# The priority of a recurrence's evictions in a hybrid diffusion layer: 60 places or 1500

## The chip, the cores and the metric

The kernel runs on one core of one Trainium2 chip. The metric is the device time of one execution in microseconds, measured over repeated runs; one further execution is taken by the hardware profiler.

## The reference

Two layers. Each projects the modulated, normalised stream into a convolution branch and a bidirectional RWKV-7 branch, joins both by an output projection and adds a SwiGLU network. Latents are 512 tokens, the context prefix 256, width 1024. What matters here is the recurrence, 8 heads of 64 by 64 state, run forwards and backwards, over the context first and from its states over the latents:

```python
def step(s, inp):
    r_t, k_t, v_t, w_t, kk_t, b_t = inp
    sa = -jnp.einsum("bhvk,bhk->bhv", s, kk_t)
    s = (s * w_t[:, :, None, :] + sa[..., None] * b_t[:, :, None, :]
         + v_t[..., None] * k_t[:, :, None, :])
    y = jnp.einsum("bhvk,bhk->bhv", s, r_t) if emit else None
    return s, y
```

```python
prep_c = rwkv_prep(uc[..., CONV_IN:], *rw)
yc, s_f, s_b = rwkv_scans(prep_c, s_zero, s_zero, emit=not last)
prep_x = rwkv_prep(ux[..., CONV_IN:], *rw)
yx, _, _ = rwkv_scans(prep_x, s_f, s_b, emit=True)
mix_x = jnp.concatenate([conformer_conv(ux[..., :CONV_IN], *cv),
                         rwkv_out(yx, prep_x, *post)], axis=-1).astype(x.dtype)
x = x + gt1 * (mix_x @ w_out[l])
x = x + gt2 * swiglu(modulate(rmsnorm(x, norm2_g[l]), sh2, sc2), ffn_wg[l], ffn_wu[l], ffn_wd[l])
```

## The kernel before

The recurrence is computed in chunks of 64 tokens. Heads come in 4 pairs, each pair has 12 chunks in 3 groups of four, so a layer has 12 blocks b (a pair and a group) and in each block 4 chain steps s, forwards and backwards side by side: 48 chain steps a layer. The stages of a block:

- `prep(b)` makes the decayed keys and receptances of a block, once for each direction: ScalarE and VectorE take turns over `tmp` and `tw` and end in `KR` and `bk`. The chunk products `grams(b)` on TensorE read these and are masked by VectorE into `G`.
- `base(b)` inverts the 16 by 16 diagonal blocks. `G` goes to memory (`d`), comes back as `Dt`, and VectorE runs 15 steps of two small instructions each (`xtmp`, then `XT`; the shapes run from 64x15 through 64x64 back to 64x15). ScalarE transposes the result, and SyncE's queue writes it to memory (`dimg`).
- `inverses` loads it as `Tm`, and `levels` extends it to 64 by 64 on TensorE, with evictions on ScalarE (`W`, `Tm`) and VectorE (`Tm`, lines 1004 and 1006).
- `tokens` turns keys and values into `tT` and `UV`.
- `chain(b, s)` is the step of the recurrence itself, and each of its matmul groups needs the eviction of the one before. `pz` (from `G` and `UV`) goes by ScalarE to `Z`; `pu` (from `Tm` and `Z`) goes by ScalarE and VectorE to the halves of `UV`; `pm` (from `tT` and `UV`) goes by VectorE to the state `S`, and two ScalarE copies put `S` into the next step's `UV`. These are the evictions that stand under `soon()`.

Beside them run the input projections (`pd` banks, evicted to `r`, `k`, `v`, `z`), the convolution, whose taps are VectorE instructions on `acc`, one for each tap (`conv`), the gating and early output projection (`mix_early`, `out_early`), and the split of each weight tile into `wh` (ScalarE) and `wl` (VectorE).

TensorE's order is written out by hand: `weave` lays all these generators into one order by a table of places, under a manual schedule of that engine alone. The order on ScalarE, VectorE, GpSimd and SyncE is set when the program is built, by a list scheduler that takes, by its own estimates of time, the ready instruction that was recorded first. `tc.high_priority(n)` lets the instructions under it count as if they had been recorded n places earlier. Each engine then runs its own instructions in that fixed order.

Of the kernel before, what the change touches and what calls it, by code (L numbers as in the profile page):

```python
# [181 lines left out]
def net(ctx: ExitStack, tc: tile.TileContext, I, out):  # L182
# [62 lines left out]
        PE.matmul(out=out, lhsT=lhsT, rhs=rhs, start=start, stop=stop)  # L245

    def soon():
        return tc.high_priority(60)

    def run(steps):  # L250
        for _ in steps:
# [350 lines left out]
    for l in range(DEPTH):  # L602
# [430 lines left out]
        def chain(b, s):  # L1033
# [18 lines left out]
            with soon():  # L1052
                act(Z, pz[:, 0:128])
# [16 lines left out]
            with soon():  # L1070
                act(UV[64:128, 2 * s_:2 * s_ + 2, 0, :], pu3[64:128], AF.Copy, scale=-1.0)
                ts(UV[0:64, 2 * s_:2 * s_ + 2, 1, :], pu3[0:64], -1.0, 0.0)
            yield

            if not fin:
                pm = bank("c")
                for d, hh in DH:
                    hs = slice(64 * hh, 64 * hh + 64)
                    mm(pm[hs, 64 * d:64 * d + 64], tT[:, hh, 2 * s_ + d, :], UV[:, 2 * s_ + d, hh, :])
                Sn = s2.tile([128, 2, 64], F32, tag="S", name=nm("S"))  # L1080
                with soon():
                    for d in range(2):
                        pd_ = pm[:, 64 * d:64 * d + 64]
                        if S is None:
                            ts(Sn[:, d, :], pd_, pc[:, d, s:s + 1], 0.0)
                        else:
                            stt(Sn[:, d, :], pd_, pc[:, d, s:s + 1], Q[:, d, :], MUL, ADD)

                    bn, sn = (b, s + 1) if s < 3 else (b + 1, 0)
                    Un = BS[bn]["UV"][sn // 2]  # L1090
                    act(Un[64:128, 2 * (sn % 2):2 * (sn % 2) + 2, 0, :], Sn[0:64])
                    act(Un[0:64, 2 * (sn % 2):2 * (sn % 2) + 2, 1, :], Sn[64:128])
                P["S"] = Sn
# [382 lines left out]
```

## Time and profile before

| | us |
|---|---|
| median of 3 runs (2222.3 to 2234.28) | 2222.33 |
| the profiled execution | 2218.84 |
| its span, first to last instruction | 2217.1 |
| mixing of layer 0, about | 140 to 620 |
| mixing of layer 1, about | 1345 to 1800 |
| VectorE, ScalarE, GpSimd busy | 1449.0, 940.3, 200.4 |

The profiled execution is 3.5 us below the median. Between the two mixing stretches lie the feed-forward network of layer 0 and the start of layer 1, and after the second one the feed-forward network of layer 1; no chain step runs there.

### The profile page before, as it was taken

The numbers are of one execution on the slowest core, as the hardware profiler recorded it, in microseconds if no ns is written. First come the engines' busy times: TensorE is split into PE (matmuls) and PEld (weight loads), VectorE is DVE, ScalarE is ACT, GpSimd is POOL, SyncE is SP. The second block draws the span as 40 slices with busy tenths as digits, with TensorE's granted clock in tenths as the row PEclk, the third lists the DMA queues.
The fourth block names the chain that finished last, engine by engine and source line by source line (L and its number), as shares of the span: only waits on it lengthen the run. The fifth ranks groups of instructions, "written<-read, shape, count | busy, mean of one in ns | idle before, by whom it ended". The sixth has DMA issues, their size and how long they took to land.

```text
span 2217.1 us, 44112 instructions
## 1 busy us (share of the span) xinstructions
PE 2057.2 (93%) x17578; PEld 1661.3 (75%) x17578; DVE 1449.0 (65%) x3286; ACT 940.3 (42%) x2184; POOL 200.4 (9%) x528
## 2 busy tenths in 40 slices
PE   5999999998998999999999999999999879999997
PEld 4777777776687888888888876667666568888886
DVE  5678888877758665565653766778877764433446
ACT  4455646555435212112112545576666443222223
POOL 0102131311010000000000000122212010000000
PEclk9999999999899999999999999999999999999998
DMA  8222232243551343343332413121214441333233
GB/s 296 70 75 71 80 78 74 65 107 117 157 195 61 123 132 126 118 139 124 122 116 92 137 40 76 32 62 47 70 33 108 123 158 58 95 97 102 86 98 121
DMA packets 197804, 226.32 MB, mean 102 GB/s; under 512 B 110560, under 2 KB 140000, under 8 KB 197472
## 3 DMA queue, kind: packets, MB, share of 16 engines
q1 hardware_dynamic: 196448, 221.42, 33.0%
q8 instruction: 138, 2.26, 0.4%
q10 hardware_dynamic: 1152, 2.10, 0.2%
q14 instruction: 66, 0.54, 0.1%
HBM read 196.62 MB, written 26.85 MB: 101 GB/s over the span
## 4 chain that ended last, share of the span: by engine, by line
PE 60%; DVE 12%; ACT 10%; issue 7%; DMA 7%; POOL 2%; SPq 0%; POOLq 0%; DVEq 0%; ACTq 0%
PE pd L245 30%; PE pw L245 23%; PE pc L245 5%; DMA at<-in_adaT 5%; ACT tmp L233 2%; DVE junk L236 2%; DVE wl L239 2%; ACT UV L233 1%; PE pw L936 1%; PE pw L412 1%; DVE acc L236 1%; ACT wh L233 1%; PE pw L924 1%; ACT W L233 1%; DVE xtmp L239 1%
## 5 line engine op out<-in xcount | busy, mean ns | idle before, releaser
L245 PE MATMUL pd<-h,wh 128*128 128x512 f32 (+3 forms) x2496 | 685.8, 364 | 10.3 <-ACT h L233 10.3
L233 ACT ACTIVATE wh<-raw 128x1024 fp32r<-128x1024 f32 (+2 forms) x234 | 220.8, 944 | 679.6 <-PE pw L245 281.1
L245 PEld LDWEIGHTS pd<-h,wh 128*128 128x128 f32 (+1 forms) x2496 | 425.9, 190 | 80.1 <-ACT h L233 11.8
L245 PE MATMUL pd<-h,wl 128*128 128x512 f32 (+3 forms) x1248 | 426.1, 364 | 2.7 <-DVE wl L239 2.7
L239 DVE TENSOR_TENSOR wl<-raw,wh 128x1024 fp32r<-128x1024 f32 (+2 forms) x234 | 253.8, 1085 | 134.6 <-ACT wh L233 133.6
L245 PE MATMUL pw<-h,wh 128*128 128x512 f32 (+1 forms) x1264 | 317.0, 350 | 3.9 <-DVE x L236 2.8
L245 PEld LDWEIGHTS pd<-h,wl 128*128 128x128 f32 (+1 forms) x1248 | 224.9, 190 | 37.7 <-DVE wl L239 3.8
L245 PEld LDWEIGHTS pw<-h,wh 128*128 128x128 f32 x1264 | 211.5, 190 | 38.9 <-DVE x L236 4.5
L236 DVE SCALAR_TENSOR_TENSOR junk<-at,cr 128x1024 bf16<-128x1024 f32 x112 | 137.0, 1224 | 130.7 <-DMA at<-in_adaT 129.4
L236 DVE SCALAR_TENSOR_TENSOR acc<-z,cw,acc 128x497 f32<-128x497 f32 (+20 forms) x216 | 193.1, 894 | 4.3 <-ACT acc L233 2.8
L245 PE MATMUL pw<-h,wl 128*128 128x512 f32 (+1 forms) x632 | 193.0, 351 | 0.0
L245 PE MATMUL pd<-mid,wh 128*128 128x512 f32 (+1 forms) x568 | 139.3, 348 | 8.5 <-ACT wh L233 2.9
L245 PE MATMUL pw<-mid,wh 128*128 128x512 f32 (+1 forms) x568 | 138.5, 347 | 1.1 <-ACT wh L233 1.1
L245 PEld LDWEIGHTS pw<-h,wl 128*128 128x128 f32 x632 | 107.4, 190 | 15.1
L245 PEld LDWEIGHTS pd<-mid,wh 128*128 128x128 f32 x568 | 94.9, 192 | 25.0 <-ACT wh L233 4.4
L245 PEld LDWEIGHTS pw<-mid,wh 128*128 128x128 f32 x568 | 95.4, 193 | 14.9 <-ACT wh L233 1.3
L1044 POOL TENSOR_TENSOR Q<-S,pc 128x128 f32<-128x128 f32 x80 | 49.5, 619 | 527.6 <-DVE S L236 210.1
L239 DVE TENSOR_TENSOR ft<-ft,pw 128x512 f32<-128x512 f32 (+1 forms) x67 | 37.7, 589 | 81.1 <-PE pw L245 80.8
L245 PE MATMUL pd<-mid,wl 128*128 128x512 f32 (+1 forms) x284 | 88.5, 351 | 2.3 <-DVE wl L239 2.2
L245 PE MATMUL pw<-mid,wl 128*128 128x512 f32 (+1 forms) x284 | 88.1, 349 | 0.2 <-DVE wl L239 0.2
L848 POOL MEMSET tmp<- 128x4 f32 x48 | 5.2, 108 | 891.5 <-PE pw L245 638.5
L239 DVE TENSOR_TENSOR xtmp<-XT,Dt 64x15 f32<-64x15 f32 (+4 forms) x360 | 74.9, 208 | 8.2 <-DMA Dt<-d 3.5
(207 smaller groups left out, 3166.5 us busy)
## 6 DMA issues: line engine op xcount, KB each, us to landing
raw<-in_wgu SPq DMA_DIRECT2D x88, 512.0 KB, 3.5
at<-in_adaT SPq DMA_DIRECT2D x56, 512.0 KB, 3.8
raw<-in_win SPq DMA_DIRECT2D x42, 512.0 KB, 3.4
ada<-in_ada SPq DMA_DIRECT2D x40, 512.0 KB, 4.7
raw<-in_wd SPq DMA_DIRECT2D x48, 320.0 KB, 2.8
Tm<-dimg SPq DMA_DIRECT2D x96, 128.0 KB, 2.8
raw<-in_wd SPq DMA_DIRECT2D x32, 384.0 KB, 3.0
d<-G SPq DMA_DIRECT2D x96, 64.0 KB, 2.1
```

The source lines that it names most:

```text
L233: A.activation(out=out, in_=in_, func=func, **k)
L236: V.scalar_tensor_tensor(out=out, in0=in0, scalar=scalar, in1=in1, op0=op0, op1=op1, **k)
L239: V.tensor_tensor(out=out, in0=a, in1=b, op=op)
L245: PE.matmul(out=out, lhsT=lhsT, rhs=rhs, start=start, stop=stop)
L412: PE.transpose(pt[:, c - c0:c - c0 + 128], wide[:, c:c + 128], ident)
L848: G.memset(lx[:, :, 0:1], 0.0)
L924: PE.transpose(pt[hh][:, o:o + 64], bk[hs, d, cc, hh:hh + 2, :].rearrange("p j t -> p (j t)"), ident[hs, hs])
L936: PE.transpose(pv[0:64, o:o + 128], src, ident)
L1044: G.tensor_tensor(out=Q, in0=S, in1=pc[:, :, s:s + 1].to_broadcast([128, 2, 64]), op=MUL)
```

## The change

The number of places by which the chain's evictions count as earlier goes from 60 to 1500. With 60 an eviction passes ready instructions that were recorded within a step or two of it; with 1500 it passes anything that is ready on its engine. No instruction is added or taken away.

```diff
     def soon():
-        return tc.high_priority(60)
+        return tc.high_priority(1500)
```

TensorE's order is the same in both kernels. Three places show what moves on the others.

ScalarE in layer 0, near 157 us. `UV<-S` are the two copies of the state, `Z` the eviction of the next step, `y` the chain's output, `z` the eviction of a projection; `tmp`, `tw` and `pc` belong to the prep of a later block. Rows with + stand there now, those with - stood there.

```order
 L233 ACTIVATE tw_1648<-pw_1644,der_147 128x256
+L233 ACTIVATE UV_1077<-S_1722 64x2x64 x2
 L233 ACTIVATE tmp_1647<-tmp_1647 128x4x64
 L233 ACTIVATE y_1555<-pc_1682 128x64 x2
+L233 ACTIVATE Z_1745<-pc_1740 128x128
 L233 ACTIVATE z_1832<-pd_1497 128x512
-L233 ACTIVATE UV_1077<-S_1722 64x2x64 x2
 L233 ACTIVATE tmp_1647<-tmp_1647 128x260 x2
-L233 ACTIVATE Z_1745<-pc_1740 128x128
+L233 ACTIVATE pc_1581<-tmp_1647 128x4
 L233 ACTIVATE tmp_1647<-tw_1648,der_147 128x4x64
-L233 ACTIVATE pc_1581<-tmp_1647 128x4
```

The copies have passed a `tmp`, the `y` pair and `z`; `Z` has passed `z` and the `tmp` pair.

VectorE in layer 1, near 1524 us, before. `XT` and `xtmp` are the inversion's steps, `bk` and the scan on `tmp` the prep's, `k` the shifted projection.

```order
L239 TENSOR_TENSOR xtmp_16276<-XT_16275,Dt_16274 64x39
L236 SCALAR_TENSOR_TENSOR bk_16520<-tw_16526,tmp_16525 128x256
L239 TENSOR_TENSOR XT_16275<-XT_16275,xtmp_16276 64x13x3
L242 TENSOR_SCALAR UV_15757<-pc_16619 64x2x64
L239 TENSOR_TENSOR xtmp_16276<-XT_16275,Dt_16274 64x28
L236 SCALAR_TENSOR_TENSOR k_16668<-pd_16338,prm,k_16668 128x511
L239 TENSOR_TENSOR XT_16275<-XT_16275,xtmp_16276 64x14x2
L236 SCALAR_TENSOR_TENSOR S_16641<-pc_16636,pc_15476,Q_16597 128x64
L239 TENSOR_TENSOR xtmp_16276<-XT_16275,Dt_16274 64x15
L236 SCALAR_TENSOR_TENSOR S_16641<-pc_16636,pc_15476,Q_16597 128x64
L239 TENSOR_TENSOR XT_16275<-XT_16275,xtmp_16276 64x15
L853 SCALAR_TENSOR_TENSOR tmp_16579<-one_95,tmp_16579 128x260
```

The same place in the changed kernel:

```order
L239 TENSOR_TENSOR xtmp_16276<-XT_16275,Dt_16274 64x55
L239 TENSOR_TENSOR bk_16520<-tmp_16525 128x4x64
L236 SCALAR_TENSOR_TENSOR S_16641<-pc_16636,pc_15476,Q_16597 128x64 x2
L239 TENSOR_TENSOR XT_16275<-XT_16275,xtmp_16276 64x11x5
L236 SCALAR_TENSOR_TENSOR bk_16520<-tw_16526,tmp_16525 128x4x64
L239 TENSOR_TENSOR xtmp_16276<-XT_16275,Dt_16274 64x48
L236 SCALAR_TENSOR_TENSOR k_16668<-pd_16338,prm,k_16668 128x511
L239 TENSOR_TENSOR XT_16275<-XT_16275,xtmp_16276 64x12x4
L236 SCALAR_TENSOR_TENSOR k_16668<-pd_16338,prm,k_16668 128x511
L239 TENSOR_TENSOR xtmp_16276<-XT_16275,Dt_16274 64x39
L853 SCALAR_TENSOR_TENSOR tmp_16579<-one_95,tmp_16579 128x260
```

The pair of `S` stood behind the `XT` of step 14 and now stands ahead of that of step 11; the last `XT` (64x15) has seventeen rows between itself and `S`.

VectorE in the last block of layer 1, near 1739 us, before. `acc` are the convolution's taps, `r` an eviction of the early output projection.

```order
L236 SCALAR_TENSOR_TENSOR S_19796<-pc_19791,pc_18597,Q_19735 128x64
L239 TENSOR_TENSOR XT_19373<-XT_19373,xtmp_19374 64x13x3
L236 SCALAR_TENSOR_TENSOR S_19796<-pc_19791,pc_18597,Q_19735 128x64
L239 TENSOR_TENSOR xtmp_19374<-XT_19373,Dt_19372 64x28
L239 TENSOR_TENSOR wl_19757<-raw_19753,wh_19755 128x768
L239 TENSOR_TENSOR XT_19373<-XT_19373,xtmp_19374 64x14x2
L236 SCALAR_TENSOR_TENSOR acc_19466<-z_18422,cw_13433,acc_19466 128x508
L239 TENSOR_TENSOR xtmp_19374<-XT_19373,Dt_19372 64x15
L236 SCALAR_TENSOR_TENSOR r_19751<-pd_19759,mod_10592,r_19751 128x512
L239 TENSOR_TENSOR XT_19373<-XT_19373,xtmp_19374 64x15
L236 SCALAR_TENSOR_TENSOR acc_19466<-z_18422,cw_13433,acc_19466 128x508
L239 TENSOR_TENSOR wl_19818<-raw_19814,wh_19816 128x768
```

The same place in the changed kernel, from `S` on:

```order
L236 SCALAR_TENSOR_TENSOR S_19796<-pc_19791,pc_18597,Q_19735 128x64 x2
L239 TENSOR_TENSOR xtmp_19374<-XT_19373,Dt_19372 64x63
L236 SCALAR_TENSOR_TENSOR acc_19466<-z_18422,cw_13433,acc_19466 128x507
L239 TENSOR_TENSOR XT_19373<-XT_19373,xtmp_19374 64x9x7
L239 TENSOR_TENSOR wl_19757<-raw_19753,wh_19755 128x768
L239 TENSOR_TENSOR xtmp_19374<-XT_19373,Dt_19372 64x60
L236 SCALAR_TENSOR_TENSOR acc_19466<-z_18422,cw_13433,acc_19466 128x508
L239 TENSOR_TENSOR XT_19373<-XT_19373,xtmp_19374 64x10x6
L236 SCALAR_TENSOR_TENSOR acc_19466<-z_18422,cw_13433,acc_19466 128x508
L239 TENSOR_TENSOR xtmp_19374<-XT_19373,Dt_19372 64x55
L236 SCALAR_TENSOR_TENSOR acc_19466<-z_18422,cw_13433,acc_19466 128x507
L239 TENSOR_TENSOR XT_19373<-XT_19373,xtmp_19374 64x11x5
```

`S` stood behind step 12 of the inversion and now stands behind step 8; sixteen more rows follow up to the last `XT` (eight of the inversion, six taps, an `r` and a second `wl`).

## Rows read from the trace of the kernel before

**Rows 1.** The page, part 1: busy time, share of the span, instructions.
```profile
PE 2057.2 (93%) x17578; PEld 1661.3 (75%) x17578; DVE 1449.0 (65%) x3286; ACT 940.3 (42%) x2184; POOL 200.4 (9%) x528
```

**Rows 2.** Windows, both mixing stretches: length, busy PE PEld DVE ACT POOL, clock, DMA.
```profile
140.00:620.00 480.00, 440.73 (x5773) 338.83 (x5773) 387.14 (x1013) 267.67 (x758) 96.90 (x224) 0.95 0.33 93
1345.00:1800.00 455.00, 414.00 (x5027) 296.24 (x5023) 327.11 (x948) 269.77 (x763) 85.06 (x234) 0.96 0.28 74
```

**Rows 3.** TensorE's waits, layer 0's mixing: us in total, times, longest.
```profile
PE pc L245 <- ACT UV L233: 9.3, 9, 1.6
...
PE pw L245 <- DVE bk L236: 4.2, 3, 1.7
...
PE pc L245 <- DVE UV L242: 1.2, 2, 0.9
```

**Rows 4.** TensorE's waits, layer 1's mixing.
```profile
PE pw L245 <- DMA Tm<-dimg: 8.1, 1, 8.1
...
PE pc L245 <- ACT UV L233: 4.3, 8, 0.9
PE pc L245 <- DVE UV L242: 4.1, 8, 0.9
PE pw L245 <- DVE bk L236: 3.8, 4, 2.1
...
PE pc L245 <- ACT Z L233: 2.4, 4, 0.7
```

**Rows 5.** Timeline near 157 us: start, us, engine, line, operation; idle time before, releaser.
```profile
155.77 0.46 DVE L236 SCALAR_TENSOR_TENSOR S<-pc,pc,Q 128x64 f32<-128x64 f32 x2
...
156.76 0.62 ACT L233 ACTIVATE z<-pd 128x512 f32<-128x512 f32 x1
...
157.40 0.64 ACT L233 ACTIVATE UV<-S 64x128 f32<-64x128 f32 x2
...
157.76 0.33 PE L245 MATMUL pc<-UV,G 128*64 128x64 f32 x2 [0.99 <-ACT UV L233]
...
161.62 0.49 PE L245 MATMUL pw<-KR,bk 64*128 64x128 f32 x2 [1.51 <-DVE bk L236]
```

**Rows 6.** Windows, a stretch of half granted clock; columns as in rows 2.
```profile
1420.20:1427.00 6.80, 6.80 (x66) 5.94 (x64) 3.75 (x8) 1.92 (x6) 0.40 (x1) 0.50 0.47 116
```

**Rows 7.** Timeline of the last block of layer 1, VectorE and TensorE.
```profile
1739.49 0.28 DVE L236 SCALAR_TENSOR_TENSOR S<-pc,pc,Q 128x64 f32<-128x64 f32 x1 [0.18 <-PE pc L245]
...
1742.70 0.16 DVE L239 TENSOR_TENSOR XT<-XT,xtmp 64x15 f32<-64x15 f32 x1
...
1743.44 0.94 DVE L239 TENSOR_TENSOR wl<-raw,wh 128x768 fp32r<-128x768 f32 x1
1744.31 8.51 DVE L236 SCALAR_TENSOR_TENSOR acc<-z,cw,acc 128x507 f32<-128x507 f32 x11
...
1750.76 1.65 PE L245 MATMUL pw<-Tm,G 64*64 64x64 f32 x16 [8.09 <-DMA Tm<-dimg]
```

**Rows 8.** Timeline, three blocks of layer 1: last XT, and TensorE's first use of Tm.
```profile
1414.49 0.15 DVE L239 TENSOR_TENSOR XT<-XT,xtmp 64x15 f32<-64x15 f32 x1
...
1426.07 0.69 PE L245 MATMUL pw<-Tm,G 64*64 64x64 f32 x8
...
1524.42 0.28 DVE L236 SCALAR_TENSOR_TENSOR S<-pc,pc,Q 128x64 f32<-128x64 f32 x1
...
1524.89 0.18 DVE L239 TENSOR_TENSOR XT<-XT,xtmp 64x15 f32<-64x15 f32 x1
...
1535.91 0.56 PE L245 MATMUL pw<-Tm,G 64*64 64x64 f32 x12
...
1634.00 0.17 DVE L239 TENSOR_TENSOR XT<-XT,xtmp 64x15 f32<-64x15 f32 x1
...
1643.69 0.68 PE L245 MATMUL pw<-Tm,G 64*64 64x64 f32 x16
```

**Rows 9.** All waits, VectorE's for the chain's banks ahead of S.
```profile
DVE S L236 <- PE pc L245: 29.8, 39, 2.0
```

## The prediction

> **What bounds the kernel now.** I read the page first, then its stretches in windows, then TensorE's own waits, then the timeline at the places where instructions move. TensorE is busy 93% of the span [rows 1]. The edit moves instructions only in the two mixing stretches, the chain's two layers, 140 to 620 us and 1345 to 1800 us: the order of every engine is the same in both kernels before and after them, and TensorE's own order is the same throughout. There TensorE is busy 440.7 of 480.0 us and 414.0 of 455.0 us [rows 2], so about 80 us of idle time is all that any reordering of the other engines could take out. VectorE is busy 387 of those 480 us, so it has little room to stand and wait.
>
> What does TensorE wait for there? The chain's evictions (UV by ScalarE, UV by VectorE, Z by ScalarE) end 9 + 2 waits of 9.3 and 1.2 us in layer 0 and 8 + 8 + 4 waits of 4.3, 4.1 and 2.4 us in layer 1: 31 waits, 21.3 us [rows 3, 4]. As much hangs on others: on bk, the last product of the prep step (4.2 and 3.8 us), and once on Tm, the block inverse that comes back through memory (8.1 us) [rows 3, 4].
>
> **The change part by part.** Nothing is added or removed; every step of the sum is a matter of who stands ahead of whom on ScalarE and VectorE.
>
> (a) *What the chain gains.* The place at 157 us shows it. The two S evictions were done at 155.77 + 0.46 = 156.23, but the copies UV<-S began at 157.40, behind z (0.62 us) and others, and TensorE stood 0.99 us for them [rows 5]. In the new order the two copies stand ahead of a tmp, the y pair and z, and would start about 1.1 us earlier, so that this wait can go. I read this off for each of the 31 waits: how late the eviction began after its input, how much work stood ahead of it then that stands behind it now, and how long TensorE waited; the smallest of the three is what it can gain. In 11 of the 31 nothing was passed. The other 20 (this is the first, the last is at 1733.5 us) give 10.1 us. **Term: -10.1 us**; ends 0, if the next wait takes it back, and -21.3, if all 31 go. I take the middle one, since it counts only work that is seen to move.
>
> The clock could add to that. The granted clock was 0.50 at 1420.2 to 1427.0 us, at full TensorE activity [rows 6], behind the waits of 1407 to 1418 us; two more such stretches of 3.4 us (from 164 and from 317.6 us) follow chain waits. If these 13.6 us ran at the upper level, 6.8 us more would go; that is put into the low end only, since the waits on bk there stay. By the Trainium skill (TensorE: Matmul & The Clock Gate, section What's actually happening) idling is what throttles the array to half rate; the trace agrees, and by that rule the sum would hold these 6.8 us, which I leave at the end of the range.
>
> (b) *What the prep step pays.* An eviction that moves up pushes others down, and here these are mostly the prep's (tmp, tw, bk). In the same place the pair of tmp (exp) and the tmp from tw fall behind UV<-S and Z, and the prep's bk is awaited by TensorE at 161.62, with 1.51 us of waiting already [rows 5]. So what the prep loses there (0.9 us by the rows) is paid in full. Of the 24 blocks TensorE takes the last bk within about 1 us of its writing in nearly all, so there is no cover. Five such places that stand alone (157, 276, 316, 398, 1704 us) add up to 0.9 + 0.8 + 2.0 + 0.9 + 1.1 = 5.7 us, if each eviction is ready no earlier than now; it will be, by what (a) gains just ahead of it, so I take half. **Term: +2.9 us**; ends 0 and +5.7.
>
> (c) *The block inverses.* A block's 15 steps of xtmp and XT run on VectorE, then go through memory (dimg) and back as Tm. In the last block of layer 1 this is visibly serial: the last XT ended at 1742.86, TensorE took the first Tm at 1750.76 after 8.09 us of standing [rows 7]. The path from the last step to TensorE is thus 7.9 us. At three places in layer 1 the lead is not much longer: 1426.07 - 1414.64 = 11.4, 1535.91 - 1525.07 = 10.8, 1643.69 - 1634.17 = 9.5 us [rows 8]; against 7.9 that is a slack of 3.5, 2.9 and 1.6 us. The new order puts S and UV evictions ahead of the last four or so steps, though the steps ran first in the trace. At 1525 us, for instance, behind S (begun at 1524.42) now come nine X operations, one bk, three k, a scan, a wl, a UV, a tmp and a tw, about 6.0 us at their durations, so the last step ends at about 1530.5, 5.4 us later. Counted alike, the others move by 4.8 and 4.9 us. Less the slack: +1.3, +2.5, +3.3. At 1414 us the prep's delay of 2.0 is the larger and takes the place of 1.3. **Term: 2.0 + 2.5 + 3.3 = +7.8 us**; ends 0, if the eviction is ready sooner by that much, and 10.8, if TensorE falls to half clock behind each (one more microsecond apiece).
>
> (d) *The last inverse.* Here there is no slack at all, and the new order is worst. Before, S stands behind step 12, and between it and the last step lie one tap of the convolution, one wl and one r; the other eleven taps follow (8.51 us, 0.77 each) [rows 7]. Now S stands behind step 8, ten taps, two wl and the r lie between S and the last step, and VectorE stands idle ahead of S, since S waits for TensorE, which is not earlier. Nine more taps at 0.77 and one more wl at 0.94 make 7.9 us; the X operations fit between the taps. So Tm comes about 8 us later, TensorE's 8.09 us become about 16, and nothing is left in its order to fill it: the next matmuls are those on Tm. **Term: +8.0 us**; ends +4, if S comes earlier by the gains of (a) and half of it is covered, and +9.
>
> Sum: -10.1 + 2.9 + 7.8 + 8.0 = **+8.6 us**. The profiled execution took 2218.84 us with a span of 2217.1, 3.5 us under the median of 2222.33; made against its own time the sum gives 2227.4, and beside the median 2231. The last is the forecast.
>
> **The rivals.** *The chain wins (A).* The gains run through: each eviction that comes earlier lets TensorE run on, which makes the next ready sooner, and the prep's and inverses' delays shrink with it. For it: all 31 waits, 21.3 us. Against: the 11 waits where nothing is passed and the 8.09 us wait. Price: -21.3 + 0 + 0 + 8 = -13, so 2209; without the last term's loss and with the clock given back, 2222.3 - 28 = 2194.
>
> *Evictions that stand and block (B), the case on the slower side.* An eviction that the order puts ahead of ready work, on an engine that takes its work in order, holds that work until its own matmul is done. VectorE already stands before S for TensorE 39 times, 29.8 us in all, with taps ready behind [rows 9]. By the Trainium skill (Perfetto Trace Analysis, section Tensor Engine Instruction) "ACT/DVE/GPSIMD are strict FIFO"; the trace agrees, as nothing passes a waiting S there, and a kernel in which that rule decides everything would take the time of this rival. The price: if none of (a) is kept and the others come at their upper ends, 0 + 5.7 + 10.8 + 9 = 25.5 us, so 2248. It decides from the point where the inverses' leads fall to 7.9 us in more than the four blocks named; of the other blocks those near 198 and 317 us come nearest.
>
> *Nothing moves on the path (C).* The moved pieces trade places in the shadow of TensorE's 93% and the sum is within 3 us of nothing: 2222. For it speaks that each single delay is one or two microseconds; against it the last inverse, which has no shadow.
>
> **How the numbers follow.** Forecast, a loss of some 4 to 20 us: 0.55. A: 0.2, of which 0.04 lies beyond 1%. B: 0.15, nearly all of it beyond 1%. C: 0.1. One per cent, 22 us, is about what a measurement of this kernel can tell from no change, and the forecast lies well inside it. Faster by over 1%: 0.04; slower by over 1%: 0.14; within: 0.82. The range leaves out the far ends of A and of B: 2209 to 2246.
>
> **What would show it.** In the new profile TensorE's waits on UV and Z should fall from 21.3 us to about 11; those on bk rise by some microseconds; the wait on Tm near the end of layer 1's mixing should be about 16 us instead of 8.1, with the eleven taps now woven between the last XT steps; and waits on Tm should appear near 1426, 1536 and 1644 us. VectorE's idle time ahead of S should grow beyond 29.8 us. The forecast is wrong if the Tm wait near 1750 us stays at 8 us (then the sum is near zero), or if the waits on UV and Z do not fall.

## The result, and the profile after

The changed kernel takes 2247.01 us (median of 5 runs, 2239.94 to 2247.87). The ratio to the kernel before is 1.0096, 95% interval 1.0077 to 1.0114: about one per cent slower. The median is 16 us above the forecast of 2231 and 1 us above the range of 2209 to 2246; taken by the ratio, 2222.33 x 1.0096 = 2243.7 us, it is inside the range. The profiled execution took 2239.94 us with a span of 2238.1, which is 21.0 us more than the 2217.1 before.

The page, part 1, of the changed kernel (to [rows 1]):

```profile
PE 2069.3 (92%) x17578; PEld 1670.3 (75%) x17578; DVE 1452.2 (65%) x3286; ACT 941.2 (42%) x2184; POOL 211.5 (9%) x528
```

The same 17578 matmul records kept TensorE busy 12.1 us longer than before. No matmul was added, so some of them ran slower; that is the first hint, and the waits alone can't show it. The other 8.9 of the 21.0 us are idle time. Of the two mixing stretches it is layer 1 where the granted clock fell, from 0.96 to 0.94 (windows to [rows 2]):

```profile
140.00:620.00 480.00, 442.06 (x5786) 339.55 (x5786) 388.31 (x1018) 267.83 (x758) 99.93 (x224) 0.95 0.33 93
1345.00:1800.00 455.00, 407.32 (x4958) 292.38 (x4958) 324.63 (x937) 267.54 (x759) 87.47 (x215) 0.94 0.26 67
```

TensorE's waits after, 140 to 640 us, for the rows shown in [rows 3] and ScalarE's bk; ahead of the colon is who waits for whom, behind it us in total, times, longest:

```profile
PE pw L245 <- DVE bk L236: 8.6, 5, 2.3
...
PE pc L245 <- ACT UV L233: 6.3, 9, 1.3
...
PE pw L245 <- ACT bk L233: 2.2, 4, 1.0
...
PE pc L245 <- DVE UV L242: 1.2, 2, 0.9
```

And 1345 to 1830 us (to [rows 4]):

```profile
PE pw L245 <- DMA Tm<-dimg: 13.7, 2, 13.4
PE pw L245 <- DVE bk L236: 11.9, 5, 3.3
...
PE pc L245 <- DVE UV L242: 2.9, 8, 0.7
...
PE pc L245 <- ACT UV L233: 1.7, 4, 0.9
PE pc L245 <- ACT Z L233: 1.0, 2, 0.5
```

The chain's waits fell from 21.3 us to 6.3 + 1.2 + 2.9 + 1.7 + 1.0 = 13.1, those for VectorE's bk rose from 8.0 to 20.5, and the one for Tm from 8.1 to 13.7. The place near 157 us shows the exchange (timeline, to [rows 5]):

```profile
157.76 0.64 ACT L233 ACTIVATE UV<-S 64x128 f32<-64x128 f32 x2
...
158.12 0.78 PE L245 MATMUL pc<-UV,G 128*64 128x64 f32 x8 [0.41 <-ACT UV L233]
...
159.11 0.61 ACT L233 ACTIVATE z<-pd 128x512 f32<-128x512 f32 x1
...
162.69 0.48 PE L245 MATMUL pw<-KR,bk 64*128 64x128 f32 x2 [2.23 <-DVE bk L236]
```

`z` now follows the copies and the chain's wait is 0.41 instead of 0.99 us; the prep's bk is waited for 2.23 instead of 1.51. The starts themselves can't be compared with those of [rows 5] directly: this execution is 1.1 us behind already at the first `pc<-UV,G` (143.1 us, before 142.0).

The price of a long wait doesn't end with it. In layer 1 TensorE waits 2.13, 3.31, 3.24 and 2.31 us for bk (its ends are at 1383.45, 1425.37, 1542.65 and 1651.90 us) and 13.41 us for Tm (to 1771.28). Windows of the changed kernel, one around or just behind each of the five; the third figure from the end is the granted clock:

```profile
1383.50:1390.30 6.80, 6.79 (x39) 5.22 (x41) 4.48 (x9) 1.22 (x4) 0.79 (x2) 0.50 0.11 22
1424.50:1441.50 17.00, 16.13 (x147) 13.97 (x148) 7.17 (x19) 4.29 (x12) 0.87 (x4) 0.50 0.30 59
1544.00:1547.40 3.40, 3.40 (x30) 2.54 (x30) 2.10 (x5) 0.93 (x4) 1.15 (x3) 0.50 0.47 84
1653.20:1656.60 3.40, 3.40 (x25) 2.44 (x26) 1.36 (x6) 0.28 (x2) 0.32 (x2) 0.50 0.39 70
1771.30:1776.00 4.70, 4.42 (x36) 3.27 (x36) 0.00 (x0) 0.38 (x1) 0.00 (x0) 0.50 0.21 59
```

That is 35.3 us at 1.2 instead of 2.4 GHz, and TensorE is busy for 34.1 of them. [Rows 6] shows the stretch of 6.8 us that stood before where now 17 us stand.

### The profile page after: what moved, and what is told of

The parts are those of the page before. It is cut to its first block, busy times and chain, and to the rows that moved or that the text cites. A ratio compares the mean times of both kernels' runs of the same rounds, so it can differ in the third digit from the quotient of the medians.

```text
span 2238.1 us, 44115 instructions
## 1 busy us (share of the span) xinstructions
PE 2069.3 (92%) x17578; PEld 1670.3 (75%) x17578; DVE 1452.2 (65%) x3286; ACT 941.2 (42%) x2184; POOL 211.5 (9%) x528
## 4 chain that ended last, share of the span: by engine, by line
PE 66%; DVE 11%; ACT 10%; DMA 6%; issue 4%; POOL 2%; SPq 0%; POOLq 0%; DVEq 0%; ACTq 0%
PE pd L245 32%; PE pw L245 26%; PE pc L245 5%; DMA at<-in_adaT 4%; ACT tmp L233 2%; DVE wl L239 2%; DVE junk L236 2%; ACT UV L233 2%; DVE acc L236 1%; PE pw L936 1%; PE pw L924 1%; ACT wh L233 1%; PE pw L412 1%; ACT G L233 1%; ACT W L233 1%
## 5 line engine op out<-in xcount | busy, mean ns | idle before, releaser
L1044 POOL TENSOR_TENSOR Q<-S,pc 128x128 f32<-128x128 f32 x80 | 58.0, 726 | 523.3 <-DVE S L236 193.0
L245 PE MATMUL pw<-KR,bk 64*128 64x128 f32 (+1 forms) x768 | 70.1, 309 | 24.2 <-DVE bk L236 21.0
```

What stands on the lines that cost most here:

```text
L1044: G.tensor_tensor(out=Q, in0=S, in1=pc[:, :, s:s + 1].to_broadcast([128, 2, 64]), op=MUL)
```

## The experiments

The question was first which part costs, then what is pushed back, then whether the clock is a cause. The table is read from each profile and each set of runs; "clock loss" is the mean over a kernel's runs of span times (1 - granted clock), in us of full clock, and takes in the half clock inside waits; waits for bk are VectorE's. Each ratio is to runs of the kernel before on the same chip, whose medians lie from 2222.3 to 2228.5 us with clock losses, where recorded, from 69.6 to 71.3.

| kernel | median us | ratio to before, 95% | waits UV, Z | bk | Tm | clock loss |
|---|---|---|---|---|---|---|
| before (run beside the four single-part kernels) | 2225.1 | 1 | 21.3 | 8.0 | 8.1 | 71.3 |
| changed | 2247.0 | 1.0096 (1.0077-1.0114) | 13.1 | 20.5 | 13.7 | 88.0 |
| ScalarE only | 2230.1 | 1.0018 (1.0001-1.0036) | 19.8 | 12.0 | 7.4 | 76.4 |
| VectorE only | 2251.1 | 1.0114 (1.0094-1.0135) | 13.9 | 22.4 | 13.8 | 93.6 |
| layer 0 only | 2226.0 | 1.0003 (0.9991-1.0015) | 17.9 | 12.2 | 7.5 | 75.4 |
| layer 1 only | 2243.0 | 1.0076 (1.0052-1.0100) | 15.0 | 16.9 | 13.8 | 86.7 |
| last inverse kept ahead | 2239.5 | 1.0058 (1.0036-1.0081) | 13.0 | 20.7 | 7.7 | 85.0 |
| all inverses kept ahead | 2241.6 | 1.0079 (1.0048-1.0110) | 15.8 | 22.7 | 7.7 | 90.0 |
| prep kept ahead | 2301.5 | 1.0329 (1.0298-1.0361) | 40.5 | 1.7 | 22.1 | 115.2 |
| prep and inverses ahead | 2241.5 | 1.0073 (1.0049-1.0097) | 42.3 | 1.7 | 7.4 | 82.5 |
| 200 places | 2246.1 | 1.0092 (1.0077-1.0107) | 14.3 | 20.8 | 10.4 | 89.7 |
| changed, waits filled | 2238.2 | 1.0058 (1.0044-1.0072) | 14.4 | 10.6 | 0.2 | 64.5 |
| before, waits filled | 2225.1 | 1.0006 (0.9992-1.0020) | 22.3 | 5.5 | none | 62.3 |
| 1500 in layer 0, filled | 2214.4 | 0.9946 (0.9924-0.9968) | 18.2 | 0.9 | 2.5 | 56.3 |

**Which part: one engine, one layer.** ScalarE's evictions alone:

```diff
-            with soon():
+            with soon(1500):
                 act(Z, pz[:, 0:128])
...
+            with soon(1500):
                 act(UV[64:128, 2 * s_:2 * s_ + 2, 0, :], pu3[64:128], AF.Copy, scale=-1.0)
-                ts(UV[0:64, 2 * s_:2 * s_ + 2, 1, :], pu3[0:64], -1.0, 0.0)
+            with soon(60): ts(UV[0:64, 2 * s_:2 * s_ + 2, 1, :], pu3[0:64], -1.0, 0.0)
```

> Z, the ScalarE half of UV and the two copies UV<-S at 1500; S and the VectorE half of UV stay at 60. VectorE's order then stays close to that of the kernel before, ScalarE's changes in a third of the places. Theory (the loss is what the chain's VectorE evictions push back there: the prep's last products and the inverse's steps): the chain's waits on ScalarE fall by some 5 us, the wait for Tm near 1750 us stays at 8 us, TensorE's waits for bk stay near 8 us in all: 2216 to 2222. Rival, displacement on ScalarE (the prep's exponentials tmp and tw are pushed back there): waits for bk rise by several microseconds, 2226 to 2235. Rival, the clock (any shift of the moments moves the half-clock stretches): anything between -7 and +7 around 2222, and not by the waits.

The chain's waits fell by 1.5 us, the bk waits rose by 4.0, and at 2230 us the rival (displacement on ScalarE) fits, though it is a small thing: the interval begins at 1.0001. The three waits together rose by only 1.8 us and the clock loss by 5.1, as much as the median, so the clock, the third reading, isn't ruled out. That this half would be a pure gain was wrong. The other half has the two numbers exchanged:

```diff
-            with soon():
+            with soon(60):
                 act(Z, pz[:, 0:128])
...
-                with soon():
+                with soon(1500):
                     for d in range(2):
```

> S and the VectorE half of UV at 1500; the three ScalarE evictions stay at 60. Theory: nearly all of the loss is here, waits for bk at 18 to 21 us instead of 8, the last wait for Tm at 13 to 16 us: 2240 to 2250, as with all at 1500. Rival, displacement on ScalarE: half of it or less, 2222 to 2233. Rival, the clock: within 7 us of 2222.

All of the loss is here, and, unexpected, nearly all of the chain's gain as well (13.9 us of waits left, 13.1 with both). ScalarE's evictions start earlier when S does, so the place of S decides for both engines.

One layer at a time, the same at all three places, and then the reverse (`1500 if last else 60`):

```diff
-            with soon():
+            with soon(60 if last else 1500):
```

> 1500 in layer 0, 60 in layer 1. Theory: layer 0 comes out even (chain waits down by 5, waits for bk up by 3, the clock about even), 2219 to 2226. Part of the 21 us arose between the mixing stretches (6.9 us from 666 to 1345 us, where the order is the same in both): if that is a consequence of when layer 0 ends, it comes back here and the time is 2226 to 2232, and if it belonged to that one execution, it doesn't. Rival, standing evictions cost everywhere: a third to a half of the loss, 2230 to 2235.

> 60 in layer 0, 1500 in layer 1. Theory: the loss of layer 1's mixing alone, +14 us: 2232 to 2240, with the wait for Tm at 13 us and waits for bk of 12 us. Rival, standing evictions cost everywhere: 2232 to 2235, with the other half in layer 0. Rival, the clock: not the sum of its parts; the excess of this run and of that with layer 0 alone don't add up to the 24 us of the medians.

Layer 0 comes out even, layer 1 alone is 0.76% slower (2243.0 us, 3 above the range expected; the waits for Tm and bk are as expected), and 0.03 + 0.76 is within the interval of the whole. Between the mixing stretches the order is the same in both kernels, yet in the profiled execution of the changed kernel 6.8 us came in there: the first grams of layer 1 began at 1319.40 instead of 1312.57, while at 655 us both were within 0.1. With layer 0 alone changed they did not come back in the median, so nothing says that the change causes them.

**What is pushed back: inverse or prep.** The steps of an inversion under the same priority, first of the last block only, then of all:

```diff
-                tt(tv, X[:, 0:n, i:i + 1].to_broadcast([64, n, m]), Dt[:, i:i + 1, i + 1:16].to_broadcast([64, n, m]), MUL)
-                tt(X[:, 0:n, i + 1:16], X[:, 0:n, i + 1:16], tv, ADD)
+                with soon(1500 if last and b == 11 else 0):
+                    tt(tv, X[:, 0:n, i:i + 1].to_broadcast([64, n, m]), Dt[:, i:i + 1, i + 1:16].to_broadcast([64, n, m]), MUL); tt(X[:, 0:n, i + 1:16], X[:, 0:n, i + 1:16], tv, ADD)
```

> All evictions at 1500 as in the changed kernel, and the inverse's 30 steps of the last block of layer 1 also at 1500 (0 elsewhere), so that S stands behind steps 12 and 13 again, one tap between it and the last step. Theory (the last inverse costs what it is late): the last wait for Tm falls from 13.4 to 8 us, the waits for bk stay at 8.6 and 11.9 us, the time falls by 5 from the changed kernel's 2247: 2240 to 2244. Rival (what is spared there is paid behind it, at the next wl or eviction): no change, 2246 to 2249.

> All evictions at 1500, the inverse's steps of all blocks at 1500 too. Theory (the inverse and the prep are both pushed back, each by the evictions): the wait for Tm falls to 8 us, the waits for bk stay near 20 us or rise, since the prep is now passed by both: 2238 to 2246. Rival (the inverse's steps, interleaved with other work, are what delays the prep): the waits for bk fall to 8 to 10 us as well, the chain's waits stay near 13 us, 2215 to 2228.

TensorE's waits from 1345 to 1830 us with all inversions kept ahead:

```profile
PE pw L245 <- DVE bk L236: 13.3, 6, 2.9
PE pw L245 <- DMA Tm<-dimg: 7.7, 1, 7.7
```

Both restore the last Tm (7.7 us). Their medians lie 7.5 and 5.4 us under the changed kernel's, about the 6 us of that wait, though the intervals still touch. Neither takes anything off the sum of the waits for bk: so these are the prep's own lateness, not that of the inversions. Now the prep under the same priority, alone, and then with the inversions:

```diff
+                with soon():
-                act(lx[:, :, 1:65], rv(pz[:, 0:256]).rearrange("p (c t) -> p c t", t=64), AF.Tanh, scale=0.5,
+                    act(lx[:, :, 1:65], rv(pz[:, 0:256]).rearrange("p (c t) -> p c t", t=64), AF.Tanh, scale=0.5,
...
-                act(pc[:, d, :], px[:, :, 64])
+                    act(pc[:, d, :], px[:, :, 64])
```

> All evictions at 1500, and the prep's instructions on ScalarE and VectorE at 1500 too, so that an eviction passes a prep step no more than it would by the order of the program. Theory: the waits for bk fall from 20.5 us to 8 or less, that for Tm stays at 13 us or grows by the prep's work ahead of the steps (up to 3 us), 2228 to 2238. Rival (the waits for bk come from VectorE standing ahead of S, whatever is passed): waits for bk stay above 15 us, 2244 to 2250.

> All evictions, the prep and the inverse's steps at 1500: only the other work (taps, wl, projections) is passed. Theory: both losses go and the gain on the chain stays, waits on UV and Z 12 to 15 us, for bk 8 or less, for Tm 8: 2210 to 2222, at or below the kernel before. Rival (the loss is in what else the evictions pass: wl, taps, projections): 2235 to 2247. Rival (the chain's gain was itself bought from prep and inverse): the waits on UV and Z back at 20 us, 2220 to 2228.

Waits with the prep alone ahead, 140 to 640 us:

```profile
PE pc L245 <- ACT UV L233: 18.1, 16, 3.7
PE pw L245 <- DVE XT L239: 8.6, 1, 8.6
PE pw L245 <- DMA Tm<-dimg: 8.5, 4, 4.0
```

Both versions take the waits for bk away (20.5 to 1.7 us), which shows what causes them (evictions that pass the prep), and both pay elsewhere. The first passes the inversions, and 2301 us refutes the forecast of 2228 to 2238. In the second the prep and the inversions are safe and the chain pays: 42.3 us of waits, twice those of the kernel before. Of its three readings the second (taps, wl and projections) has the time, 2235 to 2247, but the waits are the third's (the chain's gain is bought from prep and inversions): it expected 20 us on UV and Z, and 42.3 came. What the chain gains the prep loses, and the other way round; only the last inverse could be kept ahead with the other two as they were (13.0 and 20.7 us). Of these versions the kernel before has the least sum of the three waits, 37.4 us.

Between the two numbers:

```diff
-        return tc.high_priority(60)
+        return tc.high_priority(200)
```

> 200 places for all evictions. S then stands behind step 11 of the last inverse with three taps between it and the last step (12 or 13 and one tap with 60, 8 and ten taps with 1500); 400 places give the same order as 1500. Theory: a part of each loss, the wait for Tm 9 to 11 us, those for bk between 8 and 20 us, 2228 to 2242. Rival (the loss comes only with the far moves): 2220 to 2226, with the chain's gain kept.

It isn't between: the waits for bk and the time are those of 1500 (20.8 and 2246.1), only Tm lies between (10.4 us). The expected 2228 to 2242 was too low.

**The clock.** Extra matmuls on constants fill the five longest waits of layer 1's mixing. They only use TensorE.

```diff
-                        o = 128 * (2 * s + d)
+                        o = 128 * (2 * s + d); [mm(pg[1][:, 256:512], ident, cst[:, 0:256]) for _ in range(({2: 7, 3: 11, 6: 11, 9: 8} if last else {}).get(b, 0) if (hf, s, d) == (0, 0, 1) else 0)]
...
-            pW = bank()
+            pW = bank(); [mm(pW[:, 256:512], ident, cst[:, 0:256]) for _ in range(42 if last and b == 11 and hf == 0 else 0)]
```

> The changed kernel with extra matmuls (128x256, constant by constant, into parts of a bank that the real ones write next; 0.28 us each at the upper clock) where TensorE stands longest in layer 1: ahead of the grams of blocks 2, 3, 6, 9 (7, 11, 11 and 8 of them, for waits of 2.1, 3.3, 3.2 and 2.3 us) and ahead of the last block's first levels (42, for 13.4 us). They are no work of the reference; they fill waits. Theory that adds the clock (a long wait costs once as a wait and once more as a stretch at half clock behind it; in the changed kernel 6.8, 17.1, 3.4, 3.4 and some 6 us behind these five waits): the waits show no longer, the granted clock behind them is 1.00, and although TensorE does 22 us more the time falls by 8 to 18 us, 2229 to 2239 where the changed kernel took 2247. Rival (the wait alone is the cost, and the lower clock of the changed kernel is chance): 2245 to 2252.

Windows of this kernel, the counterpart of the stretch at 1424.50 above, and its timeline (two fills):

```profile
1423.80:1441.00 17.20, 16.95 (x227) 14.25 (x225) 10.17 (x33) 7.79 (x23) 0.94 (x4) 1.00 0.30 58
```

```profile
1423.82 5.02 PE L245 MATMUL pw<-cst 128*128 128x256 f32 x22
1428.76 0.89 PE L245 MATMUL pw<-KR,bk 64*128 64x64 f32 x12
...
1754.93 18.40 PE L245 MATMUL pw<-cst 128*128 128x256 f32 x84
```

The clock stays at 1.00, and the twelve bk matmuls take 0.89 us (1.99 in the changed kernel). Over the whole of layer 1's mixing the clock is 0.99, where the changed kernel has 0.94:

```profile
1345.00:1830.00 485.00, 455.92 (x5293) 333.16 (x5291) 345.71 (x973) 282.24 (x786) 95.82 (x240) 0.99 0.28 75
```

A matmul took 0.44 us, not 0.28, so the fills overran the waits they stand in, by 5.0 us at Tm and by 1.2 to 1.8 at the four of bk. The kernel still became 8.8 us faster (the two intervals lie apart), with TensorE doing work that the result doesn't need. The same in the kernel before (7 and 3 in blocks 2 and 3, 25 ahead of the levels):

```diff
+                        ... range(({2: 7, 3: 3} if last else {}).get(b, 0) if (hf, s, d) == (0, 0, 1) else 0)]
...
+            ... range(25 if last and b == 11 and hf == 0 else 0)]
```

> The kernel before (60) with the same extra matmuls, cut to its shorter waits: 7 ahead of the grams of block 2 (2.1 us), 3 ahead of block 3 (1.2 us) and 25 ahead of the last block's first levels (8.1 us). Theory that adds the clock: it has less to give back here (3.4, 6.8 and about 4 us at half clock behind these), so 3 to 7 us: 2218 to 2222 against 2225. Rival: no change, 2224 to 2228.

No change, which is what the rival said. The clock loss fell as the theory said, from 69.6 to 62.3 us, but the fills were too long here too: 11.06 us for a wait of 8.09, 3.29 for 2.1. By the time alone this run doesn't tell. Sized by the measured 0.44 us, and on the layer 0 version, it does:

```diff
+            with soon(60 if last else 1500):
...
+                        ... range((({2: 5, 3: 5, 5: 3, 6: 3, 8: 2}, {2: 4, 3: 2, 8: 2})[last]).get(b, 0) if (hf, s, d) == (0, 0, 1) else 0)]
...
+            pW = bank(); [mm(pW[:, 256:512], ident, cst[:, 0:256]) for _ in range(17 if last and b == 11 and hf == 0 else 0)]
```

> 1500 in layer 0 and 60 in layer 1, with the extra matmuls of the two runs before, now sized by what one took there (0.44 us: 84 records of 42 took 18.4 us, so those fills were too long by 1.0 to 5.0 us each). Ahead of the grams: 5, 5, 3, 3 and 2 in blocks 2, 3, 5, 6 and 8 of layer 0 (for waits of 2.2, 2.4, 1.4, 1.7 and 1.0 us), 4, 2 and 2 in blocks 2, 3 and 8 of layer 1 (2.1, 1.2, 0.9); ahead of the last block's first levels 17 (7.5 us). They are no work of the reference. With 1500 in layer 0 alone the time was 2226.0: the span without the half-clock loss was 4.5 us shorter than before, and 5 us more went at half clock. Theory that adds the clock: the stretches behind these waits (6.8, 3.4, 6.8, 3.4 us in layer 0, 6.8, 6.8 and some 4 in layer 1) go and give half their length back, 10 to 19 us in all less what a fill overruns: 2212 to 2220, below the kernel before (2225). Rival (the clock falls elsewhere instead): 2222 to 2228, with the granted clock of the whole run no higher than 0.968.

Its span and mean clock (the page of cores), and a window behind the first fill, where with 1500 in layer 0 alone 6.8 us ran at half clock:

```profile
core 0: 2212.7 us, clock 0.976
```

```profile
162.20:172.00 9.80, 9.61 (x100) 7.81 (x98) 9.47 (x20) 4.02 (x9) 0.52 (x2) 1.00 0.08 16
```

2214.4 us against 2228.5 for the kernel before on the same chip, ratio 0.9946 (0.9924 to 0.9968): below both kernels, as the theory that adds the clock expected. The clock loss is 56.3 us against 70.1; span times clock is 2158 against 2157 us. So the whole gain on the kernel before is the clock's. The fills did not all fit: 1.6 us of the last wait for Tm are left.

## Why the prediction was right and wrong

The mechanism of the waits was right: the change gives the chain a little and takes it from the prep and the last inversion. The size of the total was not, because the sum holds no loss of clock.

- **(a), -10.1 us for the chain's waits.** Measured: 21.3 to 13.1 us, -8.2.
- **(b) and (c), +2.9 and +7.8 us.** The sum, 10.7, was nearly met by the waits for bk (VectorE's +12.5, ScalarE's 3.9 to 3.0: +11.6). That it was met is luck, since (c) named the wrong carrier. The waits on Tm that it put near 1426, 1536 and 1644 us didn't come. At these three places TensorE stood 3.31, 3.24 and 2.31 us for the prep's bk, and with all inversions kept ahead it still stood 2.89, 2.35 and 2.40 there. The step said itself that at 1414 us the prep's delay is the larger; it is so at all three.
- **(d), +8.0 us for the last inverse.** Measured +5.3: 13.41 instead of 8.09. The order did what was read from it. Timeline of the changed kernel, to [rows 7]:

```profile
1753.99 0.48 DVE L236 SCALAR_TENSOR_TENSOR S<-pc,pc,Q 128x64 f32<-128x64 f32 x2 [0.28 <-PE pc L245]
...
1765.09 0.17 DVE L239 TENSOR_TENSOR XT<-XT,xtmp 64x15 f32<-64x15 f32 x1
...
1771.28 0.47 PE L245 MATMUL pw<-Tm,G 64*64 64x64 f32 x2 [13.41 <-DMA Tm<-dimg]
```

  From the start of S to that of the last XT pass 11.1 us, 3.2 before: 7.9 more, as counted. But from the last XT to TensorE it takes 6.0 us instead of the 7.9 that the step assumed. SyncE's queue shows where. Its rows in the kernel before:

```profile
1743.74 1.30 SPq L967 DMA_DIRECT2D dimg<-XT  x2
1745.13 0.61 SPq L323 DMA_DIRECT2D raw<-in_wo  x1
1745.84 0.38 SPq L1180 DMA_DIRECT2D r<-stash  x1
1747.09 2.58 SPq L975 DMA_DIRECT2D Tm<-dimg  x4
```

  and in the changed one:

```profile
1765.33 1.30 SPq L967 DMA_DIRECT2D dimg<-XT  x2
1768.61 2.58 SPq L975 DMA_DIRECT2D Tm<-dimg  x4
```

  `dimg` is issued 0.07 us after the last XT instead of 0.88, and TensorE starts 2.67 us after the first issue of Tm instead of 3.67. ScalarE's transpose of the last XT, here before and then changed, shows where the first of these comes from:

```profile
1743.08 0.64 ACT L233 ACTIVATE XT<-XT 64x256 f32<-64x256 f32 x1
...
1765.35 0.64 ACT L233 ACTIVATE XT<-XT 64x256 f32<-64x256 f32 x1 [7.09 <-DVE XT L239]
```

  Before, the first `dimg` was issued only as the transpose ended; now it is issued ahead of it. For the second, two other transfers were issued just ahead of Tm before; that these cost the one microsecond wasn't tried.
- **The sum.** -8.2 + 12.5 - 0.9 + 5.6 = +9.0 us of waits, where the prediction had +8.6. The term that failed is the clock. "The clock could add to that" took it for a gain, of 6.8 us at the low end; as a loss it stood only in the upper end of (c), with one microsecond behind each of three places, and the sum had it at nothing. Its reading that the stretch from 164 us follows a chain wait is doubtful too: the prep's wait of 1.51 us, which ended at 161.62 [rows 5], lies nearer. At those three places alone the half clock cost 3.4 us before (the 6.8 us of [rows 6]) and now 11.9 (17.0, 3.4 and 3.4 us, half of each).

  In the profiled execution the clock loss rose from 2217.1 x 0.030 = 66.5 to 2238.1 x 0.037 = 82.8 us, +16.3, good to some 2 us since the clocks are rounded. Laid out in windows of 1.7 us it is 23.9 us in both kernels from 140 to 655 us, 13.7 and 18.8 from 655 to 1345, and 22.2 and 32.4 from 1345 to 1860. So layer 0 lost nothing by the clock and layer 1 10.2 us. Of these 2.9 us lie in the Tm wait itself, where nothing ran (12.1 us of it at half clock against 6.4); the other 7.3 come on top of the waits. The 5.1 us between the two lie where no order changed; here are the windows of that stretch, before and changed:

```profile
640.00:1345.00 705.00, 680.38 (x3834) 587.14 (x3833) 438.17 (x761) 202.66 (x328) 10.20 (x38) 0.98 0.36 114
640.00:1345.00 705.00, 680.54 (x3782) 586.43 (x3782) 435.08 (x755) 199.10 (x321) 10.06 (x37) 0.97 0.36 113
```

  The kernel before with its waits filled, at 60 places throughout, also lost 18.8 us there in its profile, so these 5.1 can't be put down to the change. 9.0 + 7.3 + 5.1 = 21.4 us, against 21.0 measured. Over the five runs of the changed kernel the loss is 88.0 us, against 71.3 over the 23 runs of the kernel before that go with the first experiments.
- **Why it fell.** What the chain gave up were many short waits, the longest 1.6 us [rows 3]; what came were a few of 2 to 13 us, and in layer 1 most of the half clock stands at these: 47.8 of 64.9 us. By the Trainium skill (TensorE: Matmul & The Clock Gate, section What's actually happening) it is idling that throttles the array; the trace agrees, and filling the five waits left some 17 us at half clock in layer 1. A sum of waits has no place for this, and that was the error. Half clock also stood where no wait was long: layer 0, whose longest was 2.0 us before and 2.3 now, had 47.8 us of it in both kernels. Whether a microsecond in one piece costs more than one in ten pieces wasn't tried by itself.
- **The rivals.** A, the chain wins, is refuted by the time and the bk waits. B's price, 2248, is close to what was measured, but not by B's mechanism: the chain's gain was kept, and VectorE's standing ahead of S rose only from 29.8 us [rows 9] to 34.7. C is out.
- **What stays open.** What sets the length of a half-clock stretch, and why one execution gets more of them than another: single executions of one kernel differ by over 20 us along with their clock (1500 in layer 0, filled: 2209.49 us at 0.976, 2233.53 at 0.967).

## What to carry to other kernels

The sum of TensorE's waits isn't the whole price of a reordering: look at the granted clock behind each of the longer ones. Here the clock came to 10.2 us in layer 1, beside 9.0 us of waits in all, and to nothing in layer 0. A raised priority is paid by whoever is passed, so read from the order who that is and how long TensorE waits for it now; here the chain and the prep could each be made whole only at the other's cost. Where a long wait can't be removed, matmuls sized to it were worth half a per cent in one kernel (ratio 0.9946); too long by 0.4 to 3 us each, they were worth nothing in another (1.0006).

## What the runs showed of the hardware

The length of a half-clock stretch doesn't follow that of the wait: at a wait of 3.31 us TensorE ran at half the clock for 17.0 us, although it was busy 16.13 of them, and behind one of 3.24 us for 3.4 us. With matmuls in the wait of 3.31 us the clock stayed at 1.00 through the work behind it (17.20 us, of which the first 5 are the fill). A float32 matmul of 128x128 by 128x256 leaves two records and took 0.44 us (18.40 us for 84 records).
